# A hybrid decoder layer on one core: three products moved into the loop that loads x, sums of squares moved to VectorE, nine x buffers

## The chip, the cores and the metric

The kernel runs on one core of a Trainium2 chip. The metric is device time in microseconds. The engines are named as in the profile: PE (TensorE, matmuls), DVE (VectorE), ACT (ScalarE), POOL (GpSimd) and SP (SyncE, which here issues every DMA).

## What is computed

One decoder layer on x of 512 tokens by 2048 features, all in float32, and a final RMSNorm:

```python
h = rmsnorm(x, norm1_w)
proj = h @ w_in        # 6 attention heads, 4 conv groups, 6 delta-rule heads, 12 small columns
y_sb = stick_breaking_attention(heads(sb_q), heads(sb_k), heads(sb_v))
y_sc = sc_b * causal_depthwise_conv(sc_c * sc_h, sc_conv_w)
y_gdn = gdn_mixer(gdn_qkv, gdn_z, gdn_a, gdn_b, ...)   # conv, silu, l2norm, gated delta rule, gate
x = x + concat[y_sb, y_sc, y_gdn] @ w_out
h2 = rmsnorm(x, norm2_w)
x = x + square(relu(h2 @ w_up)) @ w_down
return rmsnorm(x, final_norm_w)
```

## The kernel before

x is kept transposed, as 16 tiles of 128 features by 512 tokens. Every factor of a product is split into two parts, `hi` (rounded) and `lo` (the rest), and a product is the sum of three matmuls: hi by hi, hi by lo, lo by hi (`mm3`, lines 106 to 110). `gemm(src, acts)` (lines 112 to 122) makes one product of 128 output features by 512 tokens: 4 chunks of 4 feature tiles, 12 matmuls of 512 columns per chunk, 48 in all, into one PSUM tile `mm`, of which there are three. The weights of a chunk come through `wload` (lines 96 to 104): SP issues a DMA into `raw`, ACT casts `raw` to `whi` (L102), DVE subtracts to get `wlo` (L103). `raw`, `whi` and `wlo` have four buffers each.

**The opening** (lines 175 to 217) is a loop over the 16 feature tiles k. For each, 268 weight columns are loaded (256 value columns of two attention heads and the 12 small columns) and the tile `xr` of x, of which three buffers exist. ACT makes the hi part `big` (L188), DVE the lo part (L189), PE runs 12 matmuls of 268 columns into four PSUM tiles `v` (L194 to L196). The squares of x are summed for the norm: ACT and DVE take turns to square (L204, L202), POOL adds to `acc` (L205):

```python
        else:
            sq = tmp()
            if k % 2:
                V.tensor_tensor(out=sq, in0=xr, in1=xr, op=ALU.mult)
            else:
                S.activation(out=sq, in_=xr, func=AF.Square)
            G.tensor_tensor(out=acc, in0=acc, in1=sq, op=ALU.add)
        xw.append(a)
```

After the loop PE sums `acc` over the partitions (L209, L214) and ACT makes the factors `R` (L135, L137) and `rtok`. The norm is applied after a product, so that products need `big` alone, while whoever reads a product needs `R`.

**The delta-rule stage** follows. `gdn_in(h)` (lines 355 to 395) takes three products of head h (key, query, value). Each goes through `conv_silu`: DVE multiplies the PSUM tile by `R` into `xp` (L332), which also frees that `mm` tile; then come taps on DVE (L337), a silu over ACT, DVE and POOL. Later come `kq`, and the matrices `MT` and `AT` (L390 on PE, L392 on DVE). `gdn_base(h)` inverts on DVE: `MT` is written to memory and read back rearranged (`Bq`), 62 small instructions run (L429, L431), the result goes through memory again, DVE transposes it into `X0` (L440), and PE goes on with L445. `gdn_scan(h)` is a chain of four steps over PE, DVE and ACT (L489, L491, L494, L496 and so on). Products of later heads, gates (`gdn_gate`) and conv groups (`sc_group`) lie between.

After that come attention, the output product with `w_out` (lines 733 to 753) and the MLP. The output loop loads x again into `xr` (3 buffers) and makes tiles `x1` (6 buffers), which `turn` transposes on PE later.

The order on each engine is set at build time by a scheduler with priorities (`tc.high_priority`); at run time every engine takes its instructions strictly in that order and waits at the first one that isn't ready. The scheduler may move work of a later call ahead of earlier ones.

Of the kernel before, what the change touches and what calls it, by code (L numbers as in the profile page):

```python
# [11 lines left out]
F32 = mybir.dt.float32  # L12
F32R = mybir.dt.float32r
AF = mybir.ActivationFunctionType
ALU = mybir.AluOpType
# [38 lines left out]
def trunk(ctx, tc, xT, wv1, wv2, wa, wo, wu, wd, vec, wf, out, dbg=None):  # L54
# [17 lines left out]
    def mmps():  # L72
        pool, bufs = pool_of_mm
        return pool.tile([P, 512], F32, name="mm", tag="mm", bufs=bufs)
# [21 lines left out]
    def wload(src, n, prio=None):  # L96
        with tc.high_priority(WPRIO if prio is None else prio):
            raw = per.tile([P, 512], F32, name="raw", tag="raw", bufs=4)
            nc.sync.dma_start(out=raw[:, :n], in_=src)
            hi = per.tile([P, 512], F32R, name="whi", tag="whi", bufs=4, align_bytes=256)  # L100
            lo = per.tile([P, 512], F32R, name="wlo", tag="wlo", bufs=4, align_bytes=256)
            S.copy(out=hi[:, :n], in_=raw[:, :n])  # L102
            V.tensor_tensor(out=lo[:, :n], in0=raw[:, :n], in1=hi[:, :n].bitcast(F32), op=ALU.subtract)  # L103
        return hi, lo

    def mm3(p, lh, ll, rh, rl, first, last, more=False):

        PE.matmul(p, lhsT=lh, rhs=rh, start=first, stop=False, skip_group_check=more)  # L108
        PE.matmul(p, lhsT=lh, rhs=rl, start=False, stop=False, skip_group_check=more)  # L109
        PE.matmul(p, lhsT=ll, rhs=rh, start=False, stop=last, skip_group_check=more)  # L110

    def gemm(src, acts, ts=slice(0, T)):

        p = mmps()[:, :ts.stop - ts.start]
        nk = len(acts)
        for c in range(0, nk, CHUNK_KT):
            hi, lo = wload(src[:, c:c + CHUNK_KT, :].rearrange("p k f -> p (k f)"), CHUNK_KT * P)
            for k in range(CHUNK_KT):
                s = slice(k * P, (k + 1) * P)
                a = acts[c + k]  # L120
                mm3(p, hi[:, s], lo[:, s], a[:, 0, ts], a[:, 1, ts], c + k == 0, c + k == nk - 1)
        return p

    def silu(x, s):
# [34 lines left out]
    def pt(shape, name, tag=None, bufs=1, dt=F32):  # L159
        return ph_pool.tile(shape, dt, name=name, tag=tag or name, bufs=bufs)  # L160
# [18 lines left out]
    pw = xps("r")  # L179
    for i in range(8):  # L180
        PE.matmul(pw[:, :P], lhsT=ones, rhs=ones, start=True, stop=True)
    for k in range(KT):
        hi, lo = wload(wv1[:, k, :], 268, 0)
        xr = big_pool.tile([P, 512], F32, name="xr", tag="xr", bufs=3)
        nc.sync.dma_start(out=xr, in_=xT[:, k, :])
        a = big()
        w = col(C_N1 + k)
        S.activation(out=a[:, 0], in_=xr, func=AF.Copy, scale=w)  # L188
        V.scalar_tensor_tensor(out=a[:, 1], in0=xr, scalar=w, in1=a[:, 0].bitcast(F32),  # L189
                               op0=ALU.mult, op1=ALU.subtract)  # L190
        for b in range(NB):
            s = slice(b * P, (b + 1) * P)
            mm3x = v1p[b][:, :268]
            PE.matmul(mm3x, lhsT=a[:, 0, s], rhs=hi[:, :268], start=k == 0, stop=False)  # L194
            PE.matmul(mm3x, lhsT=a[:, 0, s], rhs=lo[:, :268], start=False, stop=False)
            PE.matmul(mm3x, lhsT=a[:, 1, s], rhs=hi[:, :268], start=False, stop=k == KT - 1)  # L196
        if k == 0:
            S.activation(out=acc, in_=xr, func=AF.Square)
        else:
            sq = tmp()  # L200
            if k % 2:
                V.tensor_tensor(out=sq, in0=xr, in1=xr, op=ALU.mult)  # L202
            else:
                S.activation(out=sq, in_=xr, func=AF.Square)  # L204
            G.tensor_tensor(out=acc, in0=acc, in1=sq, op=ALU.add)  # L205
        xw.append(a)
    R = pt([P, 512], "R")
    p = xps("r")
    PE.matmul(p, lhsT=ones, rhs=acc, start=True, stop=True)  # L209
# [144 lines left out]

    def gdn_in(h):
        st = {}
        c, r = l2n(conv_silu(gemm(wa[3 * h], xw), NH + h), None)
        kq = gt([P, NB, 2, P], "kq", bufs=3)
        V.tensor_tensor(out=kq[:, :, 0], in0=c, in1=r, op=ALU.mult)
        c, r = l2n(conv_silu(gemm(wa[3 * h + 1], xw), h), lns_c)  # L360
        V.tensor_tensor(out=kq[:, :, 1], in0=c, in1=r, op=ALU.mult)
        cv = conv_silu(gemm(wa[3 * h + 2], xw), 2 * NH + h)

        vtok = ytile(1)
        p = xps("i")
        for b in range(NB):
            PE.transpose(p[:, b * P:(b + 1) * P], cv[:, b * P:(b + 1) * P], ident)
        S.copy(out=vtok, in_=p)

        G1 = [gt([P, NB, P], "g", tag="g", bufs=4, dt=F32R) for i in range(2)]  # L370
        for i in range(2):
            G.tensor_tensor(out=G1[i], in0=U32.unsqueeze(1).broadcast_to([P, NB, P]),
                            in1=ghl[:, i, :, h:h + 1].bitcast(F32).broadcast_to([P, NB, P]), op=ALU.mult)
        p = xps("i")
        for i in range(2):
            PE.matmul(p, lhsT=SLR, rhs=G1[i].rearrange("p b f -> p (b f)"), start=i == 0, stop=i == 1)
        dti = gt([P, 512], "g", tag="g", bufs=4)
        dts = gt([P, 512], "g", tag="g", bufs=4)
        S.activation(out=dti, in_=p, func=AF.Exp)
        G.affine_select(out=q4(dts), in_=q4(dti), compare_op=ALU.is_gt, fill=0.0, base=0,  # L380
                        pattern=[[0, NB], [1, P]], channel_multiplier=-1)
        G.affine_select(out=q4(dti), in_=q4(dti), compare_op=ALU.is_ge, fill=0.0, base=0,
                        pattern=[[0, NB], [1, P]], channel_multiplier=-1)
        G.tensor_tensor(out=q4(dts), in0=q4(dts), in1=be[:, :, h:h + 1].broadcast_to([P, NB, P]), op=ALU.mult)
        AT, MT = ytile(1), gt([P, 512], "MT", bufs=3)
        for c in range(2):
            p = xps("i")
            pv = p.rearrange("p (b w f) -> p b w f", b=2, w=2)
            for b in range(2):
                PE.matmul(pv[:, b], lhsT=kq[:, 2 * c + b, 0], rhs=kq[:, 2 * c + b], start=True, stop=True)  # L390
            s = slice(2 * c, 2 * c + 2)
            V.tensor_tensor(out=q4(MT)[:, s], in0=pv[:, :, 0], in1=q4(dts)[:, s], op=ALU.mult)  # L392
            V.tensor_tensor(out=q4(AT)[:, s], in0=pv[:, :, 1], in1=q4(dti)[:, s], op=ALU.mult)
        st.update(kq=kq, vtok=vtok, AT=AT, MT=MT)
        heads[h] = st
# [335 lines left out]
                       in_=p[:, h * 256:h * 256 + 256].rearrange("p (i f) -> p i f", i=2))  # L731

    for m in range(KT):
        xr = big_pool.tile([P, 512], F32, name="xr", tag="xr", bufs=3)
        nc.sync.dma_start(out=xr, in_=xT[:, m, :])
        p = gemm(wo[m], yh)
        x = big_pool.tile([P, 512], F32, name="x1", tag="x1", bufs=6)
        V.tensor_tensor(out=x, in0=p, in1=xr, op=ALU.add)
        a = xw2t([P, 2, 512], "xw2", F32R)
        w = col(C_N2 + m)  # L740
        S.activation(out=a[:, 0], in_=x, func=AF.Copy, scale=w)
        V.scalar_tensor_tensor(out=a[:, 1], in0=x, scalar=w, in1=a[:, 0].bitcast(F32),
                               op0=ALU.mult, op1=ALU.subtract)
        if m == 0:
            S.activation(out=acc2, in_=x, func=AF.Square)
        else:
            sq = tmp()
            S.activation(out=sq, in_=x, func=AF.Square)
            G.tensor_tensor(out=acc2, in0=acc2, in1=sq, op=ALU.add)
        x1.append(x)  # L750
        xw2.append(a)
        if m % 4 == 0 and m:
            turn(m // 4 - 1)
# [29 lines left out]
    def up_chunk(f, c, st):  # L783

        if c == 0:
            st["p"] = mmps()
        p = st["p"]
        hi, lo = wload(wu[f][:, c * CHUNK_KT:(c + 1) * CHUNK_KT, :].rearrange("p k f -> p (k f)"), CHUNK_KT * P)
        for k in range(CHUNK_KT):
            s = slice(k * P, (k + 1) * P)  # L790
            a = xw2[c * CHUNK_KT + k]
            mm3(p, hi[:, s], lo[:, s], a[:, 0], a[:, 1], c + k == 0, c == KT // CHUNK_KT - 1 and k == CHUNK_KT - 1)
        if c == KT // CHUNK_KT - 1:
            g = f // HK
            if f % HK == 0:
                hp[g] = mlp.tile([P, HK, 512], F32, name="hp", tag="hp", bufs=3)
            t = tmp()
            V.scalar_tensor_tensor(out=t, in0=p, scalar=0.0, in1=Rb, op0=ALU.max, op1=ALU.mult)
            S.activation(out=hp[g][:, f % HK], in_=t, func=AF.Square)
# [226 lines left out]
```

## Time and profile before

| | |
|---|---|
| median of 3 runs | 2260.18 us (2259.96 to 2262.76) |
| the profiled execution | 2259.93 us, of which 2257.9 us are the span from first to last instruction |
| busy share of PE, DVE, ACT, POOL | 98%, 73%, 41%, 9% |
| PE idle in the span | 45.1 us, of which 11.0 us in the first 50 us |
| mean granted PE clock | 0.995 |

The span counts from the first to the last instruction; the 2.0 us beyond it lie around the program. Busy time of an engine is the union of its instructions' times.

### The profile page before, as it was taken

What the parts mean: (1) busy time and instruction counts of PE and PEld (TensorE: products, weight loads), DVE (VectorE), ACT (ScalarE), POOL (GpSimd) and SP (SyncE); (2) the same over time, 40 slices, a digit from 0 to 9 for tenths busy, and PEclk for the clock granted to TensorE, in tenths of its full rate; (3) what the DMA queues carried; (4) which work ended last, traced back from release to release, by engine and by line L of the source; (5) the groups of instructions that cost most, each with busy time, mean ns of one, the idle gap of its engine ahead of it and who ended that gap; (6) DMA issues with size and microseconds to landing.
All of it is one profiled execution on the core that took longest, in us unless ns stands there. A gap on an engine that the chain in (4) does not pass through costs nothing.

```text
span 2257.9 us, 28036 instructions
## 1 busy us (share of the span) xinstructions
PE 2212.8 (98%) x10394; PEld 1834.4 (81%) x10394; DVE 1646.0 (73%) x2216; ACT 914.6 (41%) x1479; POOL 208.7 (9%) x205
## 2 busy tenths in 40 slices
PE   8999989999999999999999999999999999999998
PEld 7877777788989888788888888888888888888886
DVE  7798999854656743468787787787878878878774
ACT  5524544333434533433333333333333333333334
POOL 4323323101000111000000000000000000000003
PEclk9999999999999999999999999999999999999999
DMA  6332222333222343433433333333333243333332
GB/s 184 97 87 82 72 73 72 87 87 93 82 87 80 89 126 117 134 109 90 124 90 107 108 90 118 96 102 117 88 113 103 89 123 92 102 113 89 116 113 80
DMA packets 112504, 227.05 MB, mean 101 GB/s; under 512 B 18448, under 2 KB 20624, under 8 KB 112368
## 3 DMA queue, kind: packets, MB, share of 16 engines
q1 hardware_dynamic: 112368, 225.26, 33.8%
q8 instruction: 82, 1.34, 0.3%
q14 instruction: 54, 0.44, 0.1%
HBM read 218.53 MB, written 6.68 MB: 100 GB/s over the span
## 4 chain that ended last, share of the span: by engine, by line
PE 89%; DVE 7%; issue 1%; DMA 1%; ACT 1%; SPq 0%; POOL 0%; ACTq 0%; DVEq 0%; POOLq 0%
PE mm L108 19%; PE mm L109 19%; PE mm L110 19%; PE pp L110 8%; PE pp L108 8%; PE pp L109 8%; DVE Yq L431 2%; DVE tq L429 1%; DVE wlo L103 1%; PE mm L268 1%; PE mm L269 1%; PE mm L267 1%; DVE cv L337 1%; DVE big L189 0%; DMA xr<-in_xT_dram 0%
## 5 line engine op out<-in xcount | busy, mean ns | idle before, releaser
L102 ACT CAST whi<-raw 128x512 fp32r<-128x512 f32 (+1 forms) x544 | 333.0, 613 | 619.1 <-PE mm L109 569.5
L103 DVE TENSOR_TENSOR wlo<-raw,whi 128x512 fp32r<-128x512 f32 (+1 forms) x544 | 381.0, 701 | 233.4 <-ACT whi L102 227.3
L868 DVE TENSOR_TENSOR xq<-pp,xq 128x1024 f32<-128x1024 f32 x240 | 290.8, 1222 | 203.1 <-PE pp L110 200.6
L108 PE MATMUL mm<-big,whi 128*128 128x512 f32 x1024 | 406.4, 397 | 0.2 <-DVE y L558 0.2
L110 PE MATMUL mm<-big,wlo 128*128 128x512 f32 x1024 | 405.2, 396 | 0.2
L109 PE MATMUL mm<-big,whi 128*128 128x512 f32 x1024 | 404.4, 395 | 0.0
L108 PE MATMUL mm<-xw,whi 128*128 128x512 f32 x1024 | 398.8, 389 | 0.0
L110 PE MATMUL mm<-xw,wlo 128*128 128x512 f32 x1024 | 398.3, 389 | 0.0
L109 PE MATMUL mm<-xw,whi 128*128 128x512 f32 x1024 | 398.3, 389 | 0.0
L778 ACT CAST W<-q 128x1024 fp32r<-128x1024 f32 x210 | 220.8, 1051 | 399.4 <-PE pp L110 398.1
L108 PE MATMUL pp<-W,A 128*128 128x512 f32 x840 | 326.8, 389 | 0.0
L109 PE MATMUL pp<-W,A 128*128 128x512 f32 x840 | 326.8, 389 | 0.0
L110 PE MATMUL pp<-W,A 128*128 128x512 f32 x840 | 326.8, 389 | 0.0
L779 DVE TENSOR_TENSOR W<-q,W 128x1024 fp32r<-128x1024 f32 x210 | 255.5, 1216 | 5.3 <-ACT W L778 5.3
L110 PEld LDWEIGHTS mm<-big,wlo 128*128 128x128 f32 x1024 | 193.7, 189 | 40.6 <-DVE wlo L103 1.0
L108 PEld LDWEIGHTS mm<-big,whi 128*128 128x128 f32 x1024 | 194.0, 190 | 39.9 <-DVE y L558 0.4
L109 PEld LDWEIGHTS mm<-big,whi 128*128 128x128 f32 x1024 | 194.1, 190 | 39.7 <-DVE big L709 0.3
L108 PEld LDWEIGHTS mm<-xw,whi 128*128 128x128 f32 x1024 | 192.2, 188 | 40.3 <-issue 0.2
L109 PEld LDWEIGHTS mm<-xw,whi 128*128 128x128 f32 x1024 | 192.2, 188 | 40.1 <-issue 0.2
L110 PEld LDWEIGHTS mm<-xw,wlo 128*128 128x128 f32 x1024 | 192.0, 188 | 39.9
L110 PEld LDWEIGHTS pp<-W,A 128*128 128x128 f32 x840 | 157.8, 188 | 32.8
L109 PEld LDWEIGHTS pp<-W,A 128*128 128x128 f32 x840 | 157.6, 188 | 32.8
(264 smaller groups left out, 2226.3 us busy)
## 6 DMA issues: line engine op xcount, KB each, us to landing
raw<-in_wu_dram SPq DMA_DIRECT2D x256, 256.0 KB
q<-in_wd_dram SPq DMA_DIRECT2D x128, 512.0 KB
raw<-in_wa_dram SPq DMA_DIRECT2D x192, 256.0 KB
raw<-in_wo_dram SPq DMA_DIRECT2D x64, 256.0 KB
xr<-in_xT_dram SPq DMA_DIRECT2D x32, 256.0 KB
raw<-in_wv_dram SPq DMA_DIRECT2D x16, 256.0 KB
out_dram<-xq SPq DMA_DIRECT2D x16, 256.0 KB
raw<-in_wv_dram SPq DMA_DIRECT2D x16, 134.0 KB
```

What stands on the lines that cost most here:

```text
L102: S.copy(out=hi[:, :n], in_=raw[:, :n])
L103: V.tensor_tensor(out=lo[:, :n], in0=raw[:, :n], in1=hi[:, :n].bitcast(F32), op=ALU.subtract)
L108: PE.matmul(p, lhsT=lh, rhs=rh, start=first, stop=False, skip_group_check=more)
L109: PE.matmul(p, lhsT=lh, rhs=rl, start=False, stop=False, skip_group_check=more)
L110: PE.matmul(p, lhsT=ll, rhs=rh, start=False, stop=last, skip_group_check=more)
L267: PE.matmul(o, lhsT=xw[k][:, 0, s], rhs=hi[:, ws], start=k == 0 and b % 2 == 0, stop=False)
L268: PE.matmul(o, lhsT=xw[k][:, 0, s], rhs=lo[:, ws], start=False, stop=False)
L269: PE.matmul(o, lhsT=xw[k][:, 1, s], rhs=hi[:, ws], start=False, stop=k == KT - 1 and b % 2 == 1)
L431: V.tensor_tensor(out=Y[:, 0:i, i:32], in0=Y[:, 0:i, i:32], in1=tv, op=ALU.subtract)
L778: S.copy(out=o[:, 0], in_=src)
L779: V.tensor_tensor(out=o[:, 1], in0=src, in1=o[:, 0].bitcast(F32), op=ALU.subtract)
L868: V.tensor_tensor(out=x, in0=p, in1=x, op=ALU.add)
```

## The change

In the loop over k, after every fourth tile, one quarter (12 matmuls) of each of the first delta-rule head's three products is run, into the three `mm` tiles, which are thus all taken from the beginning. `gdn_in(0)` then uses these finished products. All squares but the first's are made by ACT as before for even k, now for all k, and DVE adds them to `acc`; POOL has no part in it. `xr` has nine buffers; in the output loop `xr` and `x1` share these nine.

```diff
-    def gemm(src, acts, ts=slice(0, T)):
...
+    def gemm_chunk(p, src, acts, c, prio=None):
+
+        ks = slice(c * CHUNK_KT, (c + 1) * CHUNK_KT)
+        hi, lo = wload(src[:, ks, :].rearrange("p k f -> p (k f)"), CHUNK_KT * P, prio)
+        for k in range(CHUNK_KT):
+            s = slice(k * P, (k + 1) * P)
+            a = acts[c * CHUNK_KT + k]
+            mm3(p, hi[:, s], lo[:, s], a[:, 0], a[:, 1], c + k == 0, c * CHUNK_KT + k == KT - 1)
+
+    def gemm(src, acts):
+        p = mmps()
+        for c in range(KT // CHUNK_KT):
+            gemm_chunk(p, src, acts, c)
         return p
...
+    first = [mmps() for _ in range(3)]
     for k in range(KT):
         hi, lo = wload(wv1[:, k, :], 268, 0)
-        xr = big_pool.tile([P, 512], F32, name="xr", tag="xr", bufs=3)
+        xr = big_pool.tile([P, 512], F32, name="xr", tag="xr", bufs=9)
...
             sq = tmp()
-            if k % 2:
-                V.tensor_tensor(out=sq, in0=xr, in1=xr, op=ALU.mult)
-            else:
-                S.activation(out=sq, in_=xr, func=AF.Square)
-            G.tensor_tensor(out=acc, in0=acc, in1=sq, op=ALU.add)
+            S.activation(out=sq, in_=xr, func=AF.Square)
+            V.tensor_tensor(out=acc, in0=acc, in1=sq, op=ALU.add)
         xw.append(a)
+        if k % CHUNK_KT == CHUNK_KT - 1:
+            for i in range(3):
+                gemm_chunk(first[i], wa[i], xw, k // CHUNK_KT, 0)
...
-        c, r = l2n(conv_silu(gemm(wa[3 * h], xw), NH + h), None)
+        prod = lambda i: first[i] if h == 0 else gemm(wa[3 * h + i], xw)
+        c, r = l2n(conv_silu(prod(0), NH + h), None)
...
-        xr = big_pool.tile([P, 512], F32, name="xr", tag="xr", bufs=3)
+        xr = big_pool.tile([P, 512], F32, name="xr", tag="xr", bufs=9)
         nc.sync.dma_start(out=xr, in_=xT[:, m, :])
         p = gemm(wo[m], yh)
-        x = big_pool.tile([P, 512], F32, name="x1", tag="x1", bufs=6)
+        x = big_pool.tile([P, 512], F32, name="x1", tag="xr", bufs=9)
```

Beside this, `up_chunk` of the MLP calls `gemm_chunk` for the same instructions as before. Lines after the loop move by 4 or 5; the text uses the numbers of before.

What this moves is set by the scheduler. The first place is PE at the end of the opening (`v` and `mm` are the PSUM tiles, `r` the column sums of the squares). Before:

```order
L196 MATMUL v<-whi,big 128x268 x4
L108 MATMUL mm<-big,whi 128x512
L109 MATMUL mm<-big,whi 128x512
...
L110 MATMUL mm<-big,wlo 128x512
L196 MATMUL v<-whi,big 128x268 x4
L209 MATMUL r<-acc,ones 128x512
L108 MATMUL mm<-big,whi 128x512
```

The same place in the change:

```order
L109 MATMUL mm<-big,whi 128x512
L110 MATMUL mm<-big,wlo 128x512
L213 MATMUL r<-acc,ones 128x512
L218 MATMUL r<-ones,acc 128x128 x4
L108 MATMUL mm<-big,whi 128x512
```

All 144 matmuls of the three products now stand before the column sum; before, 14 stood before it. The next `mm` row is the first of head 1.

The second place is DVE in the opening, after the third and around the fourth to seventh weight tile (`big` is the lo part of an x tile, `wlo` with 268 columns that of the value weights, with 512 that of a quarter). Before, five rows that go on in this manner for all k:

```order
L189 SCALAR_TENSOR_TENSOR big<-xr,vc,big 128x512
L202 TENSOR_TENSOR tmp<-xr 128x512
L103 TENSOR_TENSOR wlo<-raw,whi 128x268
L189 SCALAR_TENSOR_TENSOR big<-xr,vc,big 128x512
L103 TENSOR_TENSOR wlo<-raw,whi 128x268
```

In the change:

```order
L193 SCALAR_TENSOR_TENSOR big<-xr,vc,big 128x512
L103 TENSOR_TENSOR wlo<-raw,whi 128x512
L206 TENSOR_TENSOR acc<-acc,tmp 128x512
L193 SCALAR_TENSOR_TENSOR big<-xr,vc,big 128x512 x2
L206 TENSOR_TENSOR acc<-acc,tmp 128x512
L193 SCALAR_TENSOR_TENSOR big<-xr,vc,big 128x512
L103 TENSOR_TENSOR wlo<-raw,whi 128x268
L193 SCALAR_TENSOR_TENSOR big<-xr,vc,big 128x512
L206 TENSOR_TENSOR acc<-acc,tmp 128x512
```

The x tiles run ahead of the weights: all 16 `big` rows, 10 `acc` rows and 3 `wlo` rows of 512 columns stand before the `wlo` row of k = 7, where before one x tile and one weight tile took turns.

## Rows read from the trace of the kernel before

**Rows 1.** Part 1 of the page: busy us, share of the span, instructions.

```profile
PE 2212.8 (98%) x10394; PEld 1834.4 (81%) x10394; DVE 1646.0 (73%) x2216; ACT 914.6 (41%) x1479; POOL 208.7 (9%) x205
```

**Rows 2.** Busy by stretch: us, length, PE, PEld, DVE, ACT, POOL, clock, DMA share, GB/s.

```profile
0.00:50.00 50.00, 38.96 (x238) 34.57 (x239) 41.00 (x49) 27.67 (x52) 25.68 (x29) 1.00 0.67 192
300.00:350.00 50.00, 43.88 (x223) 35.22 (x223) 47.47 (x84) 24.72 (x51) 14.63 (x13) 0.97 0.22 64
1000.00:1050.00 50.00, 50.00 (x222) 41.42 (x221) 36.63 (x38) 17.85 (x23) 0.00 (x0) 1.00 0.37 111
```

**Rows 3.** PE's waits, whole span: for whom, us in total, times, longest.

```profile
PE v L196 <- DVE big L189: 9.3, 10, 2.3
PE s L494 <- DVE bp L491: 8.3, 4, 3.9
PE b L445 <- DVE X L440: 5.2, 2, 3.5
```

**Rows 4.** Timeline of DVE in the opening: start, us, instruction.

```profile
4.24 0.57 DVE L103 TENSOR_TENSOR wlo<-raw,whi 128x268 fp32r<-128x268 f32 x1 [3.12 <-ACT whi L102]
...
26.94 0.42 DVE L103 TENSOR_TENSOR wlo<-raw,whi 128x268 fp32r<-128x268 f32 x1
27.29 1.75 DVE L189 SCALAR_TENSOR_TENSOR big<-xr,vc,big 128x512 fp32r<-128x512 f32 x1
...
30.41 0.74 DVE L189 SCALAR_TENSOR_TENSOR big<-xr,vc,big 128x512 fp32r<-128x512 f32 x1
31.07 0.68 DVE L202 TENSOR_TENSOR tmp<-xr 128x512 f32<-128x512 f32 x1
31.67 0.42 DVE L103 TENSOR_TENSOR wlo<-raw,whi 128x268 fp32r<-128x268 f32 x1
```

**Rows 5.** Timeline of POOL in the same stretch.

```profile
27.16 3.03 POOL L205 TENSOR_TENSOR acc<-acc,tmp 128x512 f32<-128x512 f32 x2 [0.70 <-DVE tmp L202]
```

**Rows 6.** Timeline of PE, opening and first head.

```profile
36.55 0.29 PE L194 MATMUL v<-whi,big 128*128 128x268 f32 x1
...
37.42 0.29 PE L195 MATMUL v<-wlo,big 128*128 128x268 f32 x1
...
45.53 0.59 PE L209 MATMUL r<-acc,ones 128*128 128x512 f32 x1
...
78.01 0.39 PE L109 MATMUL mm<-big,whi 128*128 128x512 f32 x1
```

**Rows 7.** Busy by stretch, columns as in rows 2: for the rate of transfers.

```profile
2.00:8.00 6.00, 5.66 (x28) 5.36 (x28) 2.38 (x5) 3.79 (x11) 2.47 (x9) 1.00 0.90 267
0.00:45.50 45.50, 34.46 (x220) 31.17 (x221) 39.40 (x46) 24.97 (x48) 25.68 (x29) 1.00 0.65 187
```

**Rows 8.** Timeline of ACT and DVE: the last step of R, the first use.

```profile
47.31 0.63 ACT L137 ACTIVATE R<-R 128x512 f32<-128x512 f32 x1
...
55.70 0.69 DVE L332 TENSOR_TENSOR xp<-mm,R 128x512 f32<-128x512 f32 x1 [0.99 <-PE mm L110]
```

**Rows 9.** Busy by stretch, columns as in rows 2: from the first xp on.

```profile
55.70:101.70 46.00, 46.00 (x211) 38.08 (x210) 31.62 (x45) 26.72 (x53) 15.85 (x17) 1.00 0.33 99
55.70:161.50 105.80, 102.65 (x458) 83.95 (x456) 86.30 (x163) 48.69 (x90) 35.95 (x34) 1.00 0.32 91
55.70:420.40 364.70, 342.10 (x1681) 274.76 (x1680) 317.69 (x608) 168.42 (x330) 117.47 (x109) 0.98 0.28 81
```

**Rows 10.** Timeline of DVE and PE: inverse of the fifth head.

```profile
420.40 0.45 DVE L440 STREAM_TRANSPOSE X<-Xc 128x256 f32<-128x256 f32 x1 [4.13 <-DMA Xc<-sy]
...
421.63 0.44 PE L445 MATMUL b<-X,MT 32*32 32x32 f32 x16
```

**Rows 11.** Timeline of PE behind the wait for the first head's inverse.

```profile
162.02 0.64 PE L445 MATMUL b<-X,MT 32*32 32x32 f32 x16 [3.50 <-DVE X L440]
...
163.60 0.63 PE L108 MATMUL mm<-big,whi 128*128 128x512 f32 x1
...
166.59 0.63 PE L109 MATMUL mm<-big,whi 128*128 128x512 f32 x1
```

More of the change, by code (lines that the diff above doesn't have):

```diff
@@ L110, in mm3 @@
         PE.matmul(p, lhsT=ll, rhs=rh, start=False, stop=last, skip_group_check=more)
-    def gemm(src, acts, ts=slice(0, T)):
[L114 to L121, printed above, removed]
+    def gemm_chunk(p, src, acts, c, prio=None):
[9 more added lines that the diff above has]
+            gemm_chunk(p, src, acts, c)
         return p
@@ L356, in gdn_in @@
         st = {}
-        c, r = l2n(conv_silu(gemm(wa[3 * h], xw), NH + h), None)
+        prod = lambda i: first[i] if h == 0 else gemm(wa[3 * h + i], xw)
+        c, r = l2n(conv_silu(prod(0), NH + h), None)
         kq = gt([P, NB, 2, P], "kq", bufs=3)
         V.tensor_tensor(out=kq[:, :, 0], in0=c, in1=r, op=ALU.mult)
-        c, r = l2n(conv_silu(gemm(wa[3 * h + 1], xw), h), lns_c)
+        c, r = l2n(conv_silu(prod(1), h), lns_c)
         V.tensor_tensor(out=kq[:, :, 1], in0=c, in1=r, op=ALU.mult)
-        cv = conv_silu(gemm(wa[3 * h + 2], xw), 2 * NH + h)
+        cv = conv_silu(prod(2), 2 * NH + h)
         vtok = ytile(1)
@@ L787, in up_chunk @@
         p = st["p"]
[L788 to L792, printed above, removed]
+        gemm_chunk(p, wu[f], xw2, c)
         if c == KT // CHUNK_KT - 1:
```

## The prediction

> **What bounds the kernel now.** The page's busy shares come first: PE is busy for 98% of the span [rows 1], so only what PE waits for can be won. The stretches come next: PE idles for 11.0 of the first 50 us and again in the delta-rule stage (6.1 us in 300 to 350, where DVE is busy for 47.5 of 50); at 1000 to 1050 it is full, 222 matmuls in 50 us or 0.225 us each [rows 2]. Third the list of PE's waits: in the opening it is the lo part of x from DVE, 9.3 us in ten waits; later it is DVE again, in the scans (8.3) and the inverses (5.2) [rows 3]. Fourth the timelines, for the reason. In the opening an unhindered `big` takes 0.74 us; beside POOL's two adds (3.03 us from 27.16 on) it takes 1.75 [rows 4, 5]. So each of POOL's 15 adds costs DVE about 1 us, and DVE, not the transfers, is what PE waits for.
>
> **The change, part by part.** All sums are made in the profiled execution, 2259.93 us (2257.9 of span and 2.0 around it), 0.25 us under the median.
>
> *The mark.* I compare when PE can begin with head 1. Before, the third product's last matmuls run at 78.0 [rows 6]; by then four normalization matmuls of head 0 have run as well, about 0.9 us at 0.225 each, which now come later. Mark before: 77.1.
>
> *x and the squares.* From start to start a free DVE takes 0.35 us for a `wlo` of 268 columns, 0.66 for a `big` and 0.60 for a two-input row of 512 [rows 4]. Nothing in the trace shows an add on DVE; I price it, and a `wlo` of 512 columns, like the square of the same size, 0.60 (at least the 0.35 of half the columns, at most the 0.66 of the row with a scalar). In the new order 8 `wlo` of 268, 16 `big`, 10 adds and 3 `wlo` of 512 end with that of k = 7: 2.8 + 10.6 + 6.0 + 1.8 = 21.2 us. They begin at 4.24 [rows 4]; for the first x tiles' arrival I add 2.5 us, and get 27.9. ACT squares 8 more tiles, but it is busy for 25 of 45.5 us [rows 7] and only DVE's queue behind it matters.
>
> A rule that speaks against this move: by the Trainium skill, Perfetto Trace Analysis, section Optimizing Scalar/DVE Operations, a saturated VectorE is a reason to give work to ScalarE or even GpSimd, though it adds that the two share a read port and moving between them might not help. By its first half the ten adds would be a loss of 6.0 us on DVE; by the rows above leaving them on POOL costs some 10 us, so the move saves 4. The trace bears out the second half.
>
> *The transfers.* By then 16 x tiles, one for the output loop, 8 value weights and 3 quarters have to land: 17 and 3 of 0.262 MB and 8 of 0.137, together 6.3 MB. At 267 GB/s, the rate of 2 to 8 us, that takes 24 us from 2 on, to 26; at the opening's mean of 187 it takes 34, to 36 [rows 7]. I take 267, since the mean was held down by three buffers, and DVE's 27.9 decides; the other end costs 8 us.
>
> *The products.* From there PE has 8 tiles of 12 matmuls at 0.124 us (seven steps from 36.55 to 37.42 [rows 6]), 11.9 us, and 9 quarters of 12 at 0.225, 24.3 us, with 0.5 us for the rest of k = 7: 64.6. Per four tiles DVE needs 4 x (0.35 + 0.66 + 0.60) + 1.8 = 8.2 us against PE's 14.1, and transfers 2.4 MB or 168 GB/s, so both are covered. If that cover failed, the price would be the 8 us above.
>
> *The new wait.* The column sum now stands last, and head 1 needs an `mm` tile that only the first `xp` frees. From the sum's start to `R` took 2.4 us before (45.53 to 47.94 [rows 6, 8]); with 0.7 for `xp` and 0.1 between, head 1 begins 3.2 us after 64.6, at 67.8, and the sums fill about half of it. Behind that `xp` stand on DVE only weights of head 1. Gain at the mark: 77.1 - 67.8 = 9.3 us. Its ends are 1.3 (slow transfers) and about 13 (DVE never late).
>
> *The heads.* `R` comes 20 us later than before, and so does all the heads' work on DVE. In both orders exactly 608 DVE rows stand from the first `xp` to the transposition for the fifth head's inverse; the new ones hold six fewer `wlo` and six tiny rows more, about 3 us less. Before, this stretch took 364.7 us, 317.7 busy and 47.0 idle [rows 9]. 14.4 of the idle time lie before 101.7, where DVE waited for products that came one by one, and 19.5 before 161.5. Now three products lie ready, so I take 12 instead of 19.5, leave the later 27.5 but for 2.5, and get 37 us idle (between 25, the later part alone, and all 47). The first `xp` at 67.1 gives 67.1 + 314.7 + 37 = 418.8, and PE's L445, 1.2 us behind before [rows 10], comes at 420.0 instead of 421.6. It has 1304 product matmuls behind it instead of 1271, 33 x 0.225 = 7.4 us more. Gain there: 1.6 + 7.4 = 9.0, so the opening's gain passes through. From there on PE hardly waits, and the work left is the same.
>
> *Nine buffers in the output loop.* On SP the second x tile's load now stands behind 17 weight loads of this loop; before, the fourth's was the first to do so. Its product keeps its `mm` tile for longer, and three `mm` tiles cover that for two products of 48 x 0.225 = 10.8 us. I cost it at nothing; without that cover PE would wait at an `mm` row there, a few us once. `up_chunk` issues what it did.
>
> Sum: 2259.93 - 8.5 (between the two, rounded down for the small waits in the opening's first quarters) = 2251.4; beside the median 2251.7.
>
> **The rivals.**
> 1. *DVE's backlog eats it, and more.* If the 608 rows take the whole 364.7 us again, the fifth inverse comes at 431.8, PE's L445 at 433.0, 11.4 later and 7.4 ahead: 4.0 us lost. One more long wait such as the 3.5 us at 162 also lowers the clock: behind it matmuls start 0.427 us apart (7 steps from 163.60 to 166.59), half speed, for 11 of them, 2.2 us [rows 11]. Together 2266.4. It decides from a stretch of 360 us. For it speaks that DVE is nearly full at 300 to 350 [rows 2]; against it that a third of its idle time was waiting for the products that are now ready. Chance 0.12.
> 2. *Most is given back*, by transfers at 187 GB/s or a stretch of about 356 us: gains of 1 to 4 us, 2258. Chance 0.18.
> 3. *More is won:* with 25 us idle, PE's waits for DVE in the heads shrink as well: 12 us more, 2239. Against it: much of the idle time is round trips through memory (4.1 us at 420 [rows 10]). Chance 0.18.
>
> That the quarters do not move is excluded by the order: the first stands behind k = 3.
>
> **How the numbers follow.** The forecast has 0.52, its own range 2246 to 2256. A measurement of this kernel can tell about 0.2% from no change, 4.5 us, so faster is forecast and third rival, 0.70; same is the second, 0.18; slower the first, 0.12. The range from 2239 to 2263 takes in the second, the middle of the third and the mild half of the first.
>
> **What would show it.** Right: DVE rows of the opening at 0.74 and 0.42 us throughout; no PE wait for L189 over 1 us after 30 us; PE waiting around k = 4 to 7 for `wlo`; a PE wait of 1 to 2 us for the first `xp` near 66; PE idle in the first 70 us down to some 9 us; the fifth head's transposition at 415 to 424. Wrong: this transposition after 428, a granted clock below 0.9 in more 10 us slices than before, or `wlo` rows waiting for `raw` from memory at 20 to 36.

## The result and the profile after

| | before | changed |
|---|---|---|
| median | 2260.26 us (2259.64 to 2262.76, 6 runs) | 2269.27 us (2267.89 to 2271.14, 6 runs) |
| the profiled execution | 2259.93 us, span 2257.9 | 2267.89 us, span 2266.2 |
| PE idle in the first 50 us | 11.0 us | 2.7 us |
| first `xp` | 55.70 us | 67.16 us |
| transposition for the fifth head's inverse | 420.40 us | 431.09 us |
| PE's transpositions of the last head's output (`o`, L531; before L526) | 561.23 us | 569.40 us |

The ratio is 1.0038, with an interval from 1.0025 to 1.0051. The change is slower by 9 us. The forecast was 2251.7 us, faster; its range ended at 2263. The first rival is what came about.

Lines of the changed kernel are those of before plus 4 or 5: L193 was L189, L199 was L196, L336 was L332, L445 was L440, L450 was L445, L499 was L494. Part 1 of its page answers to [rows 1]:

```profile
PE 2216.0 (98%) x10394; PEld 1835.8 (81%) x10394; DVE 1642.9 (72%) x2223; ACT 918.8 (41%) x1487; POOL 178.8 (8%) x190
```

PE has the same 10394 matmuls; of the 8.3 us that the span is longer, 3.2 are busy time of PE and 5.1 idle time. The opening and the stretches, columns as in [rows 2]:

```profile
0.00:50.00 50.00, 47.30 (x265) 41.57 (x266) 31.81 (x58) 30.91 (x60) 3.66 (x14) 1.00 0.62 193
...
10.00:20.00 10.00, 10.00 (x52) 8.23 (x51) 10.00 (x18) 10.00 (x19) 0.00 (x0) 1.00 1.04 382
...
67.16:172.96 105.80, 103.79 (x463) 84.43 (x461) 91.36 (x173) 51.67 (x100) 35.67 (x35) 1.00 0.30 89
172.96:431.09 258.13, 230.42 (x1170) 183.17 (x1170) 229.54 (x437) 116.71 (x232) 76.60 (x75) 0.95 0.26 72
...
431.59:569.40 137.81, 131.84 (x695) 107.65 (x696) 82.98 (x164) 43.06 (x91) 10.67 (x10) 1.00 0.30 87
```

The first row is the gain: PE is busy for 47.30 of 50 us, where it was 38.96 [rows 2]. The third and fourth are where it is lost: together they are the stretch from the first `xp` to the fifth transposition, 363.9 us, against 364.7 before [rows 9], although two products that stood behind the first `xp` are now done ahead of it. The last row has 6.0 us of PE idle; before, the same stretch of the program had 0.8, as the first of these two rows of before shows (the second is for later):

```profile
421.63:561.23 139.60, 138.82 (x734) 114.58 (x734) 81.80 (x166) 44.80 (x93) 12.59 (x10) 1.00 0.32 91
...
55.70:561.23 505.53, 482.15 (x2420) 390.19 (x2419) 400.71 (x776) 213.91 (x424) 130.06 (x119) 0.98 0.30 84
```

The timeline of VectorE in the opening, which answers to [rows 4]:

```profile
9.96 0.69 DVE L206 TENSOR_TENSOR acc<-acc,tmp 128x512 f32<-128x512 f32 x1
10.56 0.43 DVE L103 TENSOR_TENSOR wlo<-raw,whi 128x268 fp32r<-128x268 f32 x1
10.91 0.75 DVE L193 SCALAR_TENSOR_TENSOR big<-xr,vc,big 128x512 fp32r<-128x512 f32 x1
...
27.19 0.44 DVE L103 TENSOR_TENSOR wlo<-raw,whi 128x268 fp32r<-128x268 f32 x1
27.54 0.69 DVE L206 TENSOR_TENSOR acc<-acc,tmp 128x512 f32<-128x512 f32 x1
```

No `big` row is stretched to 1.75 us any more; an add takes 0.60 us from start to start (9.96 to 10.56), and the `wlo` of k = 7 ends at 27.6. The timeline of all engines, PE's two waits of over 0.5 us for VectorE in the opening, and the end of it:

```profile
22.13 0.39 PE L199 MATMUL v<-wlo,big 128*128 128x268 f32 x1 [0.51 <-DVE wlo L103]
24.40 0.39 PE L199 MATMUL v<-wlo,big 128*128 128x268 f32 x1 [0.52 <-DVE wlo L103]
...
64.72 1.02 PE L213 MATMUL r<-acc,ones 128*128 128x512 f32 x2
...
66.50 0.63 ACT L140 ACTIVATE R<-R 128x512 f32<-128x512 f32 x1
66.52 1.16 PE L218 MATMUL r<-ones,acc 128*128 128x128 f32 x8 [0.78 <-ACT R L138]
...
67.16 0.69 DVE L336 TENSOR_TENSOR xp<-mm,R 128x512 f32<-128x512 f32 x1 [1.13 <-ACT R L140]
...
67.91 0.50 PE L108 MATMUL mm<-big,whi 128*128 128x512 f32 x1 [0.23 <-DVE xp L336]
```

Between the sum and head 1 PE waits 0.78 and 0.23 us. Head 1 begins at 67.91, 9.2 us ahead of the mark of before, 77.1. What PE then waits for, in the list of its waits from 67 to 600 us (for whom, us in total, times, longest):

```profile
PE b L450 <- DVE X L445: 11.6, 5, 5.2
PE s L499 <- DVE bp L496: 5.5, 4, 2.4
PE s L504 <- ACT vn L501: 2.6, 3, 1.0
PE o L531 <- DVE MT L528: 2.6, 3, 1.1
PE s L494 <- DVE Sn L509: 2.3, 2, 1.6
```

The waits for an inverse are 11.6 us in five where they were 5.2 in two [rows 3], and waits of about 1 us at many other places are new. Three of PE's rows behind an inverse, the first, the second and the fifth head's:

```profile
177.47 0.64 PE L450 MATMUL b<-X,MT 32*32 32x32 f32 x16 [5.23 <-DVE X L445]
...
226.04 0.63 PE L450 MATMUL b<-X,MT 32*32 32x32 f32 x16 [3.84 <-DVE X L445]
...
431.59 0.44 PE L450 MATMUL b<-X,MT 32*32 32x32 f32 x16 [1.04 <-DVE X L445]
```

The first answers to the 3.50 us at 162.02 [rows 11]. It comes 15.5 us later, and the wait is longer.

### The profile page after: what moved, and what is told of

The parts are those of the page before. It is cut to its first block, busy times and chain, and to the rows that moved or that the text cites. A ratio compares the mean times of both kernels' runs of the same rounds, so it can differ in the third digit from the quotient of the medians.

```text
span 2266.2 us, 28039 instructions
## 1 busy us (share of the span) xinstructions
PE 2216.0 (98%) x10394; PEld 1835.8 (81%) x10394; DVE 1642.9 (72%) x2223; ACT 918.8 (41%) x1487; POOL 178.8 (8%) x190
## 4 chain that ended last, share of the span: by engine, by line
PE 85%; DVE 10%; issue 2%; ACT 2%; DMA 1%; SPq 0%; POOL 0%; ACTq 0%; DVEq 0%; POOLq 0%
PE mm L108 18%; PE mm L109 18%; PE mm L110 18%; PE pp L108 8%; PE pp L109 8%; PE pp L110 8%; DVE tq L434 2%; DVE Yq L436 2%; DVE wlo L103 2%; DVE cv L341 1%; PE mm L273 1%; PE mm L272 1%; PE mm L271 1%; DMA Bq<-sm 0%; ACT whi L102 0%
## 5 line engine op out<-in xcount | busy, mean ns | idle before, releaser
L103 DVE TENSOR_TENSOR wlo<-raw,whi 128x512 fp32r<-128x512 f32 (+1 forms) x544 | 385.8, 710 | 242.8 <-ACT whi L102 239.2
```

## The experiments

Two numbers are read from each trace: when the first `xp` begins, and when PE transposes the last head's output (`o`). What lies between them I call the head stage. Behind a ratio to before stands its 95% interval.

### Which part of the change costs

**VectorE adds alone.** The kernel before, with the new squares and adds, three buffers and no quarters:

```diff
-            if k % 2:
-                V.tensor_tensor(out=sq, in0=xr, in1=xr, op=ALU.mult)
-            else:
-                S.activation(out=sq, in_=xr, func=AF.Square)
-            G.tensor_tensor(out=acc, in0=acc, in1=sq, op=ALU.add)
+            S.activation(out=sq, in_=xr, func=AF.Square)
+            V.tensor_tensor(out=acc, in0=acc, in1=sq, op=ALU.add)
```

> The kernel before with the squares' part of the change alone: all squares on ScalarE, all adds on VectorE, three x buffers, no quarters. Without GpSimd's adds VectorE needs 1.6 us per x tile instead of 2.4, but three buffers hold the loads back. Theory A: first xp near 50 us instead of 55.7, so 2254 to 2257. Theory C (adds on VectorE cost time): 2262 or more.

Measured: 2250.65 us against 2259.75, 0.9958 [0.9944, 0.9972]. The first `xp` comes at 47.16, 8.5 us earlier than before, and `o`, at 552.65, by 8.6; VectorE is busy for 33.95 of the first 50 us instead of 41.00. Both are better than expected (2254 to 2257, first `xp` near 50). It beats the kernel before and the changed one, and no kernel run here is clearly faster; one product in quarters (2251.23, below) is level with it. The run makes two moves at once, the squares of odd k from VectorE to ScalarE and the adds from POOL to VectorE; they were not tried apart.

**Nine buffers alone.** The kernel before with the shared nine buffers; POOL adds as it did:

```diff
-        xr = big_pool.tile([P, 512], F32, name="xr", tag="xr", bufs=3)
+        xr = big_pool.tile([P, 512], F32, name="xr", tag="xr", bufs=9)
...
-        x = big_pool.tile([P, 512], F32, name="x1", tag="x1", bufs=6)
+        x = big_pool.tile([P, 512], F32, name="x1", tag="xr", bufs=9)
```

> The kernel before with nine x buffers alone, GpSimd still adding. If VectorE beside GpSimd's adds bounds the opening, the buffers gain little: first xp 52 to 56 us, 2256 to 2260. If the loads bound it, first xp near 48 as without quarters, 2253.

Measured: 2267.79 us, 1.0034 [1.0021, 1.0046], outside what was expected. The first `xp` comes at 62.21. Its opening, by stretch and in the timeline:

```profile
0.00:50.00 50.00, 38.19 (x211) 35.72 (x211) 39.50 (x46) 24.81 (x48) 26.95 (x29) 0.83 0.54 165
```

```profile
24.14 4.09 DVE L192 SCALAR_TENSOR_TENSOR big<-xr,vc,big 128x512 fp32r<-128x512 f32 x3
24.36 3.32 POOL L208 TENSOR_TENSOR acc<-acc,tmp 128x512 f32<-128x512 f32 x2 [0.69 <-ACT tmp L207]
...
28.15 0.42 DVE L103 TENSOR_TENSOR wlo<-raw,whi 128x268 fp32r<-128x268 f32 x1
...
28.63 0.59 PE L198 MATMUL v<-wlo,big 128*128 128x268 f32 x1 [3.00 <-DVE wlo L103]
```

With more buffers the x tiles run ahead on VectorE: three `big` rows in a row, stretched by POOL's adds beside them, stand before the `wlo` that PE waits for. PE then waits 3.00 us here and 3.64 at 38.02, its granted clock is 0.83 on the mean of these 50 us (0.55 from 20 to 30 us and 0.67 from 30 to 40, where 1.00 is the level of 2.4 GHz and 0.50 that of 1.2), and fewer matmuls pass (211 against 238 [rows 2]). No run here shows the buffers to be of use: the next ones show what they do beside VectorE's adds and beside the quarters.

**The change without its quarters** (VectorE adds and nine buffers stay):

```diff
-    first = [mmps() for _ in range(3)]
...
-        if k % CHUNK_KT == CHUNK_KT - 1:
-            for i in range(3):
-                gemm_chunk(first[i], wa[i], xw, k // CHUNK_KT, 0)
...
-        prod = lambda i: first[i] if h == 0 else gemm(wa[3 * h + i], xw)
+        prod = lambda i: gemm(wa[3 * h + i], xw)
```

> Undoes one part: the first head's products are made after the x loop again; squares added on VectorE and nine buffers stay. Theory A (the delta-rule stage takes a fixed time of about 364 us from the first xp to the fifth head's transposition, 364.7 before and 363.9 in the change, so the end follows the start of that stage): the value columns end near 33 us, first xp near 45 instead of 55.7 and 67.2, so 2250 to 2253. Theory B (the time is lost because the scheduler put the heads' instructions in a worse order, whatever the start): the order of before returns, so the opening's gain of PE alone counts, 2250 to 2252, but the first xp would not tell. Both expect it faster than before; theory C (VectorE adds or nine buffers cost the time) expects 2265 or more.

Measured: 2253.59 us, 0.9972 [0.9960, 0.9983]; first `xp` at 48.74, `o` at 554.44. Theory C is out: in the change it is neither the adds nor the buffers that lose the time. Between A and B the run does not decide, since both gave about this time; the first `xp` came later than the 45 of theory A. The quarters cost 15.7 us. The buffers, beside VectorE's adds, cost some 3 us (against the kernel with the adds alone), of which the profiled executions show 1.8 by `o`.

**The change with three buffers again** (and six of `x1`):

```diff
-        xr = big_pool.tile([P, 512], F32, name="xr", tag="xr", bufs=9)
+        xr = big_pool.tile([P, 512], F32, name="xr", tag="xr", bufs=3)
...
-        x = big_pool.tile([P, 512], F32, name="x1", tag="xr", bufs=9)
+        x = big_pool.tile([P, 512], F32, name="x1", tag="x1", bufs=6)
```

> The changed kernel with three x buffers instead of nine (and six for x1 as before): quarters of all three products and VectorE adds. Beside the sixth experiment it adds the quarters alone. Theory A: the sum still stands behind all 144 matmuls, PE has nothing to idle for, first xp 64 to 67 us, so 2267 to 2271; if the nine buffers were what spoils the changed kernel, about 2255.

Measured: 2268.04 us, 1.0032 [1.0020, 1.0044]; first `xp` at 65.88, `o` at 568.35. The loss does not hang on the buffers: with nine, 2269.27 was measured, and the two kernels' runs overlap. Step by step from the kernel before to the changed one, the adds give 9.1 us, the buffers then cost 2.9 and the quarters then 15.7. These are differences along one path, so that they add up proves nothing, and they hang on what is there already: the buffers alone cost 8.0 us, beside the adds 2.9, and beside adds and quarters 1.2.

### What in the quarters costs

**Only one of the three products in quarters:**

```diff
-    first = [mmps() for _ in range(3)]
+    first = [mmps()]
...
-            for i in range(3):
+            for i in range(1):
                 gemm_chunk(first[i], wa[i], xw, k // CHUNK_KT, 0)
...
-        prod = lambda i: first[i] if h == 0 else gemm(wa[3 * h + i], xw)
+        prod = lambda i: first[i] if h == 0 and i == 0 else gemm(wa[3 * h + i], xw)
```

> Only the first of the three products runs in quarters beside the value columns; the other two follow the sum as before. Its 48 matmuls are 10.9 us, about what PE idles in the opening before. Theory A: value columns and this product end near 42, first xp near 45, 2249 to 2252. Theory B: the order of the heads decides; with an order like the changed kernel's (the normalization matmuls stand as there) 2262 or more.

Measured: 2251.23 us, 0.9961 [0.9948, 0.9973]; first `xp` at 47.61 (expected near 45), `o` at 554.45. One product ahead of the sum, as in the kernel with the adds alone, is harmless.

**The column sum early**, all three products in quarters, the sum and `R` at a high priority:

```diff
-    p = xps("r")
-    PE.matmul(p, lhsT=ones, rhs=acc, start=True, stop=True)
-    rsqrt_exp(R, p, 1.0 / D, None)
+    with tc.high_priority(CPRIO):
+        p = xps("r")
+        PE.matmul(p, lhsT=ones, rhs=acc, start=True, stop=True)
+        rsqrt_exp(R, p, 1.0 / D, None)
```

> The changed kernel with one thing moved: the column sum of the squares and R get a high priority, so that they run as soon as the last square is added (near 34 us) and the first product can be used when its last quarter is done, near 60 us, instead of after all three. The order of the heads stays close to the changed kernel's. Theory A: first xp 7 us earlier than in the change, so 2262 to 2264. Theory B: the order is still the worse one, 2268 to 2270.

Measured: 2264.06 us, 1.0015 [1.0006, 1.0024]; first `xp` at 60.20, `o` at 563.61. The first `xp` comes 7.0 us earlier than in the changed kernel, `o` 5.8 and the end 5.2. `R` is done at 40.21, but the first `xp` waits on until the first product ends, whose quarters run in turn with those of the other two. The fifth head's transposition does not follow. It comes at 431.80, where it came at 431.09, so that the stretch which the expectations called fixed, some 364 us, is 371.6 here; what follows the first `xp` is `o`. The time is what theory A gave and not theory B's 2268 to 2270, but the order of the heads did not stay close to the changed kernel's, as had been expected (546 of 773 of VectorE's rows, counted as explained below), so this run alone does not exclude theory B.

**One product and the sum early**, the two edits above together (with `rtok` under the priority too):

> One product in quarters as in the third experiment, and the sums of the squares and R and rtok at high priority, so that they are ready before this product ends. Theory A: first xp near 45.3 instead of 47.6, 2249 to 2251, the fastest so far or level with the third experiment. If the first xp is not what counts, no change from 2251.

Measured: 2252.39 us, 0.9966 [0.9953, 0.9978]; first `xp` at 47.70 where 45.3 was expected. `R` is done at 38.84, and the first `xp` waits for the product instead, where it waited 1.13 us for `R` with the sum in its old place. With one product ahead, moving the sum wins nothing.

**No quarters, but the three products whole and ahead of the sum:**

```diff
-        if k % CHUNK_KT == CHUNK_KT - 1:
-            for i in range(3):
-                gemm_chunk(first[i], wa[i], xw, k // CHUNK_KT, 0)
+    first = [gemm(wa[i], xw) for i in range(3)]
     R = pt([P, 512], "R")
```

> No quarters, but all three products are put ahead of the column sum, behind the x loop. PE has the same work done at the sum as in the change, and the first xp comes near 68 us. Theory A: as slow as the change, 2268 to 2272, though no product runs beside the value columns. If the quarters beside the value columns themselves were the cost (their weights delaying the value weights), 2258 to 2262.

Measured: 2273.43 us, 1.0056 [1.0044, 1.0069]; first `xp` at 71.65, `o` at 575.31; the time and the first `xp` are a little later than expected. The quarters as such are not needed for the loss; the place of the three products before the sum is enough.

### What paces the head stage

In all kernels so far the head stage takes 502 to 507 us, whatever was done before it. The scheduler builds the order anew for each kernel, so I counted VectorE's rows of the stage that stand in the same order in two traces (the longest such sequence, by operation and tiles). The kernel before and those with adds alone, nine buffers alone, no quarters, one product, and one product with the sum early have almost one order: each of the five shares at least 751 of the 776 rows of before. Their first `xp` lies between 47.16 and 62.21, and their head stage between 505.5 and 506.8 us. The changed kernel, three buffers and the products whole have another order, at least 713 of 773 rows the same; their first `xp` lies between 65.88 and 71.65, and their head stage between 502.2 and 503.7. Within each order the end follows the first `xp`. The question is why the second, with two products fewer behind the first `xp`, takes only some 3 us less. Either VectorE paces it from the first `xp` on, or something else. Four kernels take VectorE rows out of the heads, in two ways, from a kernel with a late first `xp` and from one with an early one.

**Two taps, on the changed kernel.** It leaves out one of the three taps that VectorE adds in each product of the heads, 18 rows of some 0.8 us up to the fifth inverse:

```diff
-        for i in (2, 1, 0):
+        for i in (2, 1):
```

> The changed kernel without one of the three convolution taps of every delta-rule product (18 VectorE rows fewer, with a mean of 0.82 us before, 12 to 14 us of VectorE's time in the stage); nothing else is left out, and PE's work is the same. If VectorE's queue paces the stage (theory A), the stretch from the first xp to the fifth transposition falls from 364 us to some 352 and the time to 2256 to 2261. If round trips through memory and PE's order pace it, 2266 or more.

Measured: 2254.58 us against 2259.75 of before, 0.9975 [0.9965, 0.9986]: 14.7 us less than the changed kernel, and a little less than the 2256 to 2261 expected. The stretch to the fifth transposition is 349.8 us.

**A shorter silu, on the kernel with VectorE adds alone.** One ScalarE and one VectorE row less in each:

```diff
-        S.activation(out=s, in_=x, func=AF.Abs)
-        S.activation(out=s, in_=s, func=AF.Exp, scale=-1.0)
+        S.activation(out=s, in_=x, func=AF.Exp, scale=-1.0)
...
-        V.scalar_tensor_tensor(out=s, in0=x, scalar=0.0, in1=s, op0=ALU.min, op1=ALU.subtract)
-        S.activation(out=s, in_=s, func=AF.Exp)
+        S.activation(out=s, in_=s, func=AF.Exp, scale=-1.0)
```

> The sixth experiment's kernel (VectorE adds alone) with one VectorE row less per silu: exp(-ln(1+exp(-x))) on ScalarE in three rows instead of four with a VectorE row between them, the same function. Some 23 rows of about 0.7 us leave VectorE in the stage, 13 to 16 us. If VectorE paces the stage, 2235 to 2240, faster than both kernels; if the late start alone was the point and the stage is bound otherwise once it starts early, 2248 to 2251.

Measured: 2251.53 us against 2260.54, 0.9959 [0.9946, 0.9971]. Nothing was won against the 2250.65 without this edit; the expectation, 2235 to 2240, was wrong. Either taps pace the heads and silu rows do not, or it is the kernel under the edit that decides. The last two runs cross the edits and the kernels.

**Two taps, on the kernel with VectorE adds alone** (the same tap left out):

> The kernel of e6 (VectorE adds the squares, no quarters) with two of the convolution's three taps: it leaves out the tap with i = 0 in each head's three silu products, as e5 did on the changed kernel. e5 gave 14.7 us and a stretch from the first xp to the fifth transposition of 349.8 us instead of 363.9; the shorter silu of e10, on the kernel of e6, gave nothing. Theory A, the base decides (a late start leaves the heads paced by VectorE, an early one by the round trips between engines): removing VectorE work from the early-start kernel gives nothing again, the stretch stays at 360 to 364 us and the time at 2248 to 2251. Theory B, the kind of work decides (the taps stand in each head's own chain from product to kq): the stretch falls by 13 to 15 us to about 350, the time to 2235 to 2239.

Measured: 2250.64 us against 2260.47, 0.9958 [0.9946, 0.9971]; nothing won.

**The shorter silu, on the changed kernel:**

> The changed kernel with the silu of e10: exp(-ln(1 + exp(-x))), which takes one VectorE row and one ScalarE row out of each silu and computes the same function for inputs of this size. On the kernel of e6 it gave nothing (2251.53 against 2250.65; stretch 360.8). Theory A, the base decides: with the late start of the changed kernel VectorE paces the heads, its 13.6 us less come off the stretch (350) and the time falls from 2269.3 to 2254 to 2257. Theory B, the kind of work decides: the stretch stays at 360 to 364 us and the time at 2267 to 2270.

Measured: 2258.41 us, 0.9992 [0.9983, 1.0001]: 10.9 us less than the changed kernel, a little short of what theory A gave (2254 to 2257) and far from theory B (2267 to 2270). In time theory A holds in both runs: the kernel under the edit decides. The stretches to the fifth transposition lie between the theories: 358.1 us with two taps on the early kernel (A 360 to 364, B 350) and 356.2 here (A 350, B 360 to 364).

| less VectorE work by | early first `xp` (2250.65) | late first `xp`, three products ahead (2269.27) |
|---|---|---|
| one tap | 2250.64, nothing | 2254.58, 14.7 us |
| one silu row | 2251.53, nothing | 2258.41, 10.9 us |

The head stage shows what goes with it, in one row of the stretches view for each kernel, columns as in [rows 2]. The kernel with VectorE adds alone, then the same with two taps, then with the shorter silu:

```profile
47.16:552.65 505.49, 481.51 (x2421) 390.05 (x2420) 401.45 (x782) 215.64 (x431) 130.01 (x119) 0.98 0.29 84
```

```profile
47.98:551.68 503.70, 479.78 (x2412) 387.04 (x2411) 383.24 (x763) 216.41 (x430) 123.43 (x119) 0.98 0.28 83
```

```profile
47.70:555.92 508.22, 485.57 (x2433) 394.93 (x2432) 384.94 (x760) 204.95 (x409) 124.22 (x119) 0.98 0.29 84
```

The changed kernel, then the same with two taps, then with the shorter silu:

```profile
67.16:569.40 502.24, 466.06 (x2328) 375.25 (x2327) 404.38 (x773) 211.44 (x423) 122.94 (x119) 0.97 0.28 80
```

```profile
67.31:554.93 487.62, 460.97 (x2328) 371.80 (x2327) 383.23 (x755) 211.57 (x423) 122.05 (x119) 0.99 0.29 82
```

```profile
66.57:557.95 491.38, 464.94 (x2329) 375.80 (x2327) 375.90 (x750) 198.68 (x400) 120.08 (x119) 0.97 0.28 82
```

With an early first `xp`, PE has about 2420 matmuls in the head stage, 482 us of work, and idles for 22.7 to 24.0 us, whether VectorE works 401 us or 383. With a late one it has 2328 matmuls, 92 fewer (two products are 96), 466 us; but it idles for 36.2 us, and only with less VectorE work does that fall, to 26.7 and 26.4. Read so, there are two limits. PE's own order gives about 505 us with 2420 matmuls, and by an estimate from these rows would give about 490 with 2328 (466 and the same 24), which is where the two kernels with a late start and less VectorE work arrive (487.6 and 491.4). VectorE's work gives 502 to 504, counted from the first `xp`, in all four kernels that have done all three products, or most of them, by then (the changed one, three buffers, the sum early, the products whole). The kernel before, whose row for this stage stands with its others above (505.53 us, 2420 matmuls, 23.4 us idle), sits on the first limit, but the second is 3 us below it. Nine buffers alone have a late first `xp` too (62.21) but 2420 matmuls behind it, and PE idles for 22.9 us as in the early kernels: lateness alone does not divide the two columns; what is done ahead, or the order that comes with it, does.

A rival stays open: the order. Each of the four edits changed the order of the head stage together with VectorE's work. With two taps and with the shorter silu, 543 and 539 of VectorE's rows stand in the changed kernel's order (of its 773), and 532 and 530 in that of the kernel with VectorE adds alone (of 782). Two different edits, in different orders, gave nearly the same in each column, which speaks for the work; a run that takes work away and keeps the order was not made. The pages' chains that ended last (part 4) agree only in part: VectorE has 7% of the span on it before and 10% in the changed kernel, 4% in the latter with the shorter silu, but still 9% with two taps. So that the stage did not get shorter is measured, and that VectorE's amount of work holds it is likely, but not shown.

What makes up the 23 to 24 us that PE idles even with less VectorE work was not tried and stays open. The waits for `bp` (8.3 us) and for the inverses (5.8) lead the list in the kernel with VectorE adds alone, much as before [rows 3].

## Why the prediction was wrong

**Right, to a few tenths:** everything up to head 1.
- *x and the squares:* the `wlo` of k = 7 ends at 27.6 (forecast 27.9), an add takes the 0.60 us that I took from the nearest row, and no `big` row is stretched. The run with VectorE's adds alone, which takes POOL's adds to VectorE and the squares of odd k to ScalarE, won 9.1 us, and all of its `big` rows take 0.74 or 0.75 us, against 1.75 beside POOL's adds before [rows 4, 5]. The Trainium skill, Perfetto Trace Analysis, section Optimizing Scalar/DVE Operations, names ScalarE, or even GpSimd, as a place to move a saturated VectorE's work to, and adds that GpSimd and VectorE share a read port, so that moving work between these two might not help. This run agrees: squares moved to ScalarE and adds taken off GpSimd won together; what either gave alone was not tried.
- *The transfers:* 382 GB/s at 10 to 20 us, more than the 267 that I took, and no row of VectorE from 9 to 30 us waits for anything.
- *The products* and *the new wait:* the sum starts at 64.72 (64.6), `R` is done at 67.13, the first `xp` comes at 67.16 (67.1), head 1 at 67.91 (67.8). The gain at the mark is 9.2 us (9.3). (The 8.5 that the sum then takes lies under both gains, 9.3 and 9.0, that it is said to lie between.)
- *Nine buffers in the output loop*, costed at nothing: from 575 to 2230 us PE is busy for 1652.91 us, in the like 1655 us of before for 1652.90. Beside VectorE's adds the nine buffers cost some 3 us in all, by the comparison above; I had priced the opening whole.

**Wrong: the step *The heads*.** It took the stretch from the first `xp` to the fifth transposition at 314.7 us busy and 37 idle. Measured were 320.9 busy (91.36 + 229.54) and 43.0 idle (14.4 and 28.6), so the transposition came at 431.09, not 418.8, beyond the 428 that I had named as proof against it. A second sign of being wrong came as well: six 10 us slices have a granted clock below 0.9, before four. The third, `wlo` rows that wait for memory at 20 to 36 us, did not. Of the 12.2 us that this term was short, half is idle time and half is work.
- Idle: the three ready products did save VectorE waits at first, 19.5 us to 14.4 in the first 105.8 us. But I had put these at 12, and I also took 2.5 off the later 27.5, which became 28.6. The list of VectorE's waits, of before from 55 to 421 us and of the changed kernel from 67 to 432, shows the round trips through memory at each inverse (for whom, us in total, times, longest):

```profile
DVE X L440 <- DMA Xc<-sy: 11.2, 5, 4.1
DVE tq L429 <- DMA Bq<-sm: 3.5, 2, 2.6
```

```profile
DVE X L445 <- DMA Xc<-sy: 14.6, 4, 4.7
DVE tq L434 <- DMA Bq<-sm: 5.1, 4, 1.7
```

Together they grew from 14.7 us to 19.7, although three products lay ready.

- Work: six `wlo` fewer should have saved 3 us. There are 95 of them in this stretch instead of 101, but each took longer. The group in the list by form, of the changed kernel from 67.16 to 431.09 and of before from 55.70 to 420.40 (count, busy us, mean ns, idle before):

```profile
L103 DVE TENSOR_TENSOR wlo<-raw,whi 128x512 fp32r<-128x512 f32 x95 | 75.8, 799 | 4.2 <-ACT whi L102 3.4
```

```profile
L103 DVE TENSOR_TENSOR wlo<-raw,whi 128x512 fp32r<-128x512 f32 x101 | 73.9, 731 | 12.3 <-ACT whi L102 11.1 <-DMA raw<-in_wa_dram 0.3
```

What lengthens them was not tried. The idle column shows the idle time before these rows shrink from 12.3 to 4.2 us. The round trips took 5.0 of these 8.1 us back, and the whole idle time fell only from 47.0 to 43.0.

**Wrong as well: *From there on PE hardly waits.*** Between the fifth inverse and `o` PE idles for 6.0 us, before 0.8. The two add up: PE's L450 came 11.6 us later than forecast (431.59 for 420.0) and 5.2 us went behind it, 16.8 together; the sum of 2251.4 and these is 2268.2, and the profiled execution took 2267.9.

**What I had missed behind both.** I followed the gain of the opening as if PE alone would carry it to the end, and gave VectorE's stretch a shorter time because its idle time looked like waiting for products. By the rows above the heads were balanced: PE's limit lies 3 us above the second, which is likely VectorE's. Running two more products ahead of the first `xp` takes 16 us of PE's busy time out of the head stage, but `xp` then comes 11.5 us later than before and 20 later than VectorE's adds allow, and the head stage, counted from it, gives back only 3. The order showed the sum behind all 144 matmuls, and I wrote that `R` comes 20 us later; its price stood in the trace, in the 47 idle us out of 364.7 [rows 9]: VectorE had little to catch up with.

**The first rival** named this mechanism, with a stretch of 364.7 us against 363.9 measured, and 2266.4 us (beside the median). It decided, as said there, above 360. Its 4.0 us for the late inverse were 2.6 (L450 came 10.0 us later, with 7.4 us of products done ahead). The one more long wait with a lower clock that it priced at 2.2 us took another form: 5.2 us of small waits behind the fifth inverse. Together that is 7.8 us, and the profiled execution took 8.0 more than before. Its chance of 0.12 was too small: nothing in the rows excluded it but my reading of the idle time.

## What to carry to other kernels

When work is pulled ahead on the engine that is busiest, ask when the other engines' chain then starts. Here the end of the head stage followed the first row that reads `R` by 502 to 507 us in every kernel until VectorE's work behind it was cut; so what releases that chain (a column sum of 2.4 us and the first product) belongs before the long thing that merely fills PE (144 matmuls, 32 us); with the sum alone moved, and the first product still in quarters among the others, only 5.2 of 15.7 us came back. And whether an engine is near its limit is tested by taking work off it in both kernels: the same edits were worth nothing in one and 11 to 15 us in the other. Where a scheduler sets the order anew, such a test should also hold the order, which it did not here.

## What the runs showed of the hardware

- More buffers alone made the kernel 8.0 us slower, with an order in which VectorE's longer rows, stretched beside POOL's adds, stand ahead of those that PE needs; PE's granted clock was 0.83 over the first 50 us, where it had been 1.00.
- The DMA engines moved 382 GB/s over 10 us of the opening, at a mean share of 1.04; the highest rate in the trace before that I had used was 267.
- Matmuls cost more at a lower granted clock: the head stage's 2328 matmuls took 466.06 us at a mean of 0.97 and 460.97 at 0.99. How long PE idles does not settle it: with the shorter silu it idles for 26.4 us, with two taps for 26.7, and its 2329 matmuls took 464.94 us at 0.97.
